# Splitting the next quarter's token norm over the output products, and reading a scan's carry from its own tile

## The chip, the core and the metric

The kernel runs on one NeuronCore of one Trainium2 chip. The metric is the device time of one execution in microseconds (us). Five engines work beside each other, each through its own queue in program order: TensorE (PE, with its weight loads as PEld), VectorE (DVE), ScalarE (ACT), GpSimd (POOL) and SyncE (SP), which here issues nearly all DMAs. They wait for each other by semaphores.

## What is computed

One layer of a hybrid decoder on 2048 tokens of width 1024 with 16 meta tokens in front, all in float32. In short:

```python
xn   = rms_norm(h, norm_w)                    # h: meta tokens, then x
proj = xn @ w_in                              # 72 chunks of 128 columns, and two small ones
o_sb = stick_breaking_attention(q, k, v)      # 4 heads of 128
o_gd = gated_delta_rule_chunked(...)          # 4 heads
o_hg = hgrn2_chunked(...)                     # 4 heads
y    = sum over the three branches b of sigmoid(mix_b) * (o_b @ w_branch[b])
out  = h + y @ w_out
```

In stick-breaking attention a query's weight on a key is sigmoid(z) times the product of sigmoid(-z) over the keys between them. Keys are worked through backwards, block by block, and the running product at a block's first key is the start value (the carry) of the next block:

```python
log_keep   = where(mask, log_sigmoid(-z), 0)
log_passed = cumsum(log_keep, reverse) - log_keep
attn       = where(mask, exp(log_sigmoid(z) + log_passed), 0)
```

## The kernel before

**Tiles and quarters.** Features lie on the 128 partitions, tokens on the free axis. The tokens are worked in four quarters of 512 (`TQ`). A product that needs float32 accuracy is three matmuls (`mm3`, lines 158 to 160): each operand is split into a high part (a cast) and a low part (the rest, by `sub_lo`, line 118). So a weight half of 128x512 is loaded raw (line 146, the tile `wraw`, two buffers), cast on ACT (line 147, `w`), its low part formed on POOL or DVE (line 118), and both parts are written back to device memory for later quarters (line 151, `wk`); from the second quarter on they are loaded ready (line 140).

**A quarter.** `dense_work` yields the dense part in small steps: the projections of attention, delta rule and HGRN2, the gates and products of the three branches (`branch`), and last the output product (`outp`, eight products e = 0 to 7 of 24 matmuls each). The scans of the three branches are separate generators, and `weave` runs them between the steps of the dense part.

**The end of a quarter.** The last branch (b = 2) ends each of its eight products like this: DVE multiplies the PSUM result with the gate (line 1188) and adds y (line 1192), ACT casts the sum to `yh` (line 1194), and POOL forms `yl` (line 118, `S<-D,y`). A PSUM tile of these products is free again after line 1188; `p_acc` has three buffers `acc`, and for part of a quarter one more, `av`. Beside it `norm_stats` loads the next quarter's x (eight tiles `D`) and forms the row factor `rb`. Then `norm_x` (lines 258 to 273) makes the next quarter's normed tokens in one go, eight steps k = 0 to 7, each of three instructions: a multiply on DVE (line 264), a cast to `xh` on ACT (line 269), and the low part `xl` on DVE, or on POOL for k = 2 and 5 (line 118). After it `outp` runs; for each e it loads weights and a piece of x into a tile `D` (line 1215, on SP), adds the finished product on DVE (line 1221) and stores it (line 1222).

**The scan.** `sb_scan` works for each head over blocks of keys; `weights` does, for each of four query tiles i: scores on PE, two sigmoids on ACT into `pc` and `at` (lines 512 and 513), the start value of the block put into the extra column of `pc` by POOL (line 517), a running product over `pc` on DVE (line 518), a copy of its last value, column 0, into a small tile `cc` on DVE (line 523), and the product `at` times `pc` on DVE or POOL (line 526). The scan takes its start value from `cc`, and so does the POOL copy. `pc`, `at` and other tiles share 21 buffers of the pool `S`.

**What sets the order.** The code gives a program order; a scheduler at build time then orders each engine's queue by that order and by a model of when operands and buffers come free. `tc.issue_after(ins)` puts what its block records behind the instruction `ins` in the queue of that instruction's engine; it adds no wait between engines.

Of the kernel before, what the change touches and what calls it, by code (L numbers as in the profile page):

```python
# [7 lines left out]
F32 = mybir.dt.float32  # L8
# [3 lines left out]
ALU = mybir.AluOpType  # L12
# [3 lines left out]
P = 128  # L16
# [23 lines left out]
def kernel(  # L40
# [21 lines left out]
    nc = tc.nc  # L62
# [193 lines left out]
    marks = {}  # L256

    def norm_x(j, xt, rb):

        c0 = META  # L260
        xh, xl = [], []
        for k in range(KC):
            t = xt[k]
            nc.vector.scalar_tensor_tensor(
                t[:, c0:], t[:, c0:], nw[:, k : k + 1], rb[:, c0:], ALU.mult, ALU.mult
            )
            h_ = xpool.tile([P, WQ], F32R, tag=f"xh{k}", name=nm("xh"))
            l_ = xpool.tile([P, WQ], F32R, tag=f"xl{k}", name=nm("xl"))
            nc.scalar.copy(h_[:, c0:], t[:, c0:])
            sub_lo(l_[:, c0:], t[:, c0:], h_[:, c0:], nc.gpsimd if k % 3 == 2 else nc.vector)  # L270
            xh.append(h_)
            xl.append(l_)
        return xh, xl

    CHUNK_US = 5.3
    STEP = 1
# [214 lines left out]
    def sb_scan(j, h, st):  # L491

        qh, ql, kh, kl, vh, vl, vm0, rq, gate = st.pop(h)
        av = p_av()
        carry = [None] * NT
        started = [False]

        def weights(s, lo, hi, skh, skl, ats):
            for i in range(NT):
                e = min(hi, META + (i + 1) * P) if s == j else hi  # L500
                if e <= lo:
                    continue
                n = e - lo
                z = p_z()
                diag = s == j and e == META + (i + 1) * P
                qs = slice(META + i * P, META + (i + 1) * P)
                mm3(z[:, :n], qh[:, qs], ql[:, qs], skh[:, lo:e], skl[:, lo:e], True, not diag)
                if diag:
                    nc.tensor.matmul(z[:, n - P : n], ident_b, neg_b, start=False, stop=True)
                pc = slot("S")  # L510
                at = slot("S")
                nc.scalar.activation(pc[:, :n], z[:, :n], AF.Sigmoid, scale=rq[:, NT + i : NT + i + 1])  # L512
                nc.scalar.activation(at[:, :n], z[:, :n], AF.Sigmoid, scale=rq[:, i : i + 1])  # L513
                if carry[i] is None:
                    nc.gpsimd.memset(pc[:, n : n + 1], 1.0)
                else:
                    nc.gpsimd.tensor_copy(pc[:, n : n + 1], carry[i])
                nc.vector.tensor_tensor_scan(  # L518
                    pc[:, 0:n][:, ::-1], pc[:, 0:n][:, ::-1], zero1.broadcast_to([P, n]),
                    1.0 if carry[i] is None else carry[i], ALU.mult, ALU.add,  # L520
                )
                cc = slot("cc", (P, 1), F32, 10)
                nc.vector.tensor_copy(cc, pc[:, 0:1])
                carry[i] = cc
                eng = nc.gpsimd if i % 2 else nc.vector
                eng.tensor_mul(at[:, :n], at[:, :n], pc[:, 1 : n + 1])  # L526
                ats[i] = at
                yield 0.4 + n * 0.0045

        def values(s, work, svh, svl, vm, final):  # L530
            def product(wi, ath, atl):
                lo, ats, a, kw, kt = work[wi]
                cs_ = slice(kt if (s == j and kt is not None) else 0, None)
                cs_ = slice(cs_.start * P, TQ)
                if kt is None:
                    lh, ll = vm
                else:
                    lh, ll = svh[:, kt * P : (kt + 1) * P], svl[:, kt * P : (kt + 1) * P]
                mm3(
                    av[:, cs_], lh, ll, ath[:kw, cs_], atl[:kw, cs_], not started[0],  # L540
                    final and wi == len(work) - 1,
                )
                started[0] = True

            left = None
            for wi, (lo, ats, a, kw, kt) in enumerate(work):
                i0 = kt if (s == j and kt is not None) else 0
                tr = p_tr()
                for i in range(i0, NT):
                    nc.tensor.transpose(tr[:kw, i * P : (i + 1) * P], ats[i][:, a - lo : a - lo + kw], ident)  # L550
                ath = slot("S", (P, TQ), F32R)
                atl = slot("S", (P, TQ), F32R)
                cs_ = slice(i0 * P, TQ)
                nc.scalar.copy(ath[:kw, cs_], tr[:kw, cs_])  # L554
                sub_lo(atl[:kw, cs_], tr[:kw, cs_], ath[:kw, cs_], nc.vector)
                if left:
                    product(*left)
                left = (wi, ath, atl)
                yield 0.7
            product(*left)  # L560
            yield 0.1

        before = None
        work = []
        for s in range(j, -1, -1):
            vm = vm0
            if s == j:
                skh, skl, svh, svl = kh, kl, vh, vl
            else:
                cs = 0 if s == 0 else META  # L570
                skh = slot("S", dt=F32R)
                skl = slot("S", dt=F32R)
                svh = slot("S", (P, TQ), F32R)
                svl = slot("S", (P, TQ), F32R)
                dd = d_kv[(s, h, "k")] + d_kv[(s, h, "v")]
                for t_, d_ in ((skh, dd[0]), (skl, dd[1])):
                    nc.sync.dma_start(t_[:, cs:].bitcast(F32), d_[:, cs:])
                for t_, d_ in ((svh, dd[2]), (svl, dd[3])):
                    nc.sync.dma_start(t_.bitcast(F32), d_)
                if s == 0:  # L580
                    vm = [slot("vmh", (META, HD), F32R, 2), slot("vml", (META, HD), F32R, 2)]
                    for t_, d_ in zip(vm, dd[4:]):
                        nc.sync.dma_start(t_.bitcast(F32), d_)
            for lo, hi in [(META + 2 * P, WQ), (0, META + 2 * P)] if s == 0 else [(META, WQ)]:
                ats = {}
                now = weights(s, lo, hi, skh, skl, ats)
                if before is None:
                    yield from now
                else:
                    yield from alternate(now, before)  # L590
                if lo == 0:
                    work.append((lo, ats, 0, META, None))
                for kt in range(NT):
                    if lo <= META + kt * P < hi:
                        work.append((lo, ats, META + kt * P, P, kt))
                if s == j == 0 and lo > 0:
                    continue
                if s == j:
                    work.sort(key=lambda w_: -1 if w_[4] == 0 else (0 if w_[4] is None else w_[4]))
                before = values(s, work, svh, svl, vm, lo == 0)  # L600
                work = []
        yield from before
        return put_ob(av, gate)
# [560 lines left out]
    def branch(j, xs, b, obs, y, yh, yl, lag=0):  # L1164
# [10 lines left out]
        def product(e):  # L1175
# [8 lines left out]
            if b == 0:  # L1184
                y[e] = slot("y", (P, TQ))
                nc.vector.tensor_mul(y[e], g, ps)
            else:
                nc.vector.tensor_mul(g, g, ps)  # L1188
                if b == 1:
                    nc.gpsimd.tensor_add(y[e], y[e], g)  # L1190
                else:
                    nc.vector.tensor_add(g, y[e], g)
                    yh[e] = slot("y", (P, TQ), F32R)
                    nc.scalar.copy(yh[e], g)
                    yl[e] = slot("S", (P, TQ), F32R)
                    sub_lo(yl[e], g, yh[e])

        for i in range(KC + lag):
            if i < KC and lag:
# [8 lines left out]
                yield from product(e)  # L1208
            yield END

    def outp(j, yh, yl):
        for e in range(KC):
            wh, wl = load_w(w_out[e], ("out", e))
            xt = slot("D", (P, TQ))
            nc.sync.dma_start(xt, xq[j, :, e, META:])
            ps = p_acc()
            for k in range(KC):
                mm3(ps, wh[k], wl[k], yh[k], yl[k], k == 0, k == KC - 1)
                if k % STEP == STEP - 1 and k < KC - 1:
                    yield 1.3  # L1220
            nc.vector.tensor_add(xt, xt, ps)
            nc.sync.dma_start(out[j, e], xt)
            yield END

# [36 lines left out]
    def dense_work():  # L1261

        xs = norm_x0()
        for j in range(nq):
# [23 lines left out]
            if j + 1 < nq:  # L1288
                xn = norm_stats(j + 1)
            yield from b2  # L1290
            if j + 1 < nq:
                xs = norm_x(j + 1, *xn)
            yield from outp(j, yh, yl)
        flush()

    dense = dense_work()
# [205 lines left out]
```

## Time and profile before

| | |
|---|---|
| median of 3 executions | 2868.03 us (2866.24, 2868.03, 4574.48) |
| profiled execution | 2863.85 us, span of its instructions 2861.6 us |
| granted TensorE clock, mean | 0.995 |
| busy, share of the span | PE 98%, PEld 81%, DVE 53%, ACT 33%, POOL 26% |
| DMA queue of SP | 519.98 MB, 55.9% of 16 engines |
| attention scans | 216, of which 152 start from a carry |
| steps of the norm in question | 3 quarters x 8 |

The profile is of one execution. A group row gives line, engine, operation, tiles (result<-operands), shapes and count, then busy time, mean of one in ns, and the idle time of its engine just before such instructions with what ended it. A row of the waits gives who waited for whom, total us, times and longest. A row of the timeline gives start, duration, engine, line and tiles, with idle time ahead in brackets. A row of a stretch gives its length, the busy time of each engine with the number of instructions, the granted TensorE clock, the share of the DMA engines and GB/s. The busy time of PE is modelled from pipelined matmuls. Line numbers are those of the kernel before; behind the change they are one to five off.

### The profile page before, as it was taken

Reading aid. Unit: us, or ns where it says so; the run is one execution under the profiler, and the core shown is the slowest. Engines: PE = TensorE matmul, PEld = TensorE weight load, DVE = VectorE, ACT = ScalarE, POOL = GpSimd, SP = SyncE. Lnnn points to the kernel's source line nnn. Section 1 sums busy time; section 2 is a strip of 40 time slices with the busy share of each in tenths; the row PEclk is TensorE's granted clock in tenths of the full one; section 3 lists DMA queues with packets and bytes.
Section 4 is the critical chain, followed back from the end, with each engine's and each line's share of the span. In section 5 each row is a group of like instructions: output and inputs, shape, how many; then the busy total and the mean of one; then the engine's idle time right before and its main releaser. Section 6 shows DMA issues by size and latency. Waiting matters only on the chain.

```text
span 2861.6 us, 42199 instructions
## 1 busy us (share of the span) xinstructions
PE 2793.7 (98%) x15720; PEld 2327.8 (81%) x15720; DVE 1523.8 (53%) x3089; ACT 933.8 (33%) x2131; POOL 753.2 (26%) x1009
## 2 busy tenths in 40 slices
PE   7999999998999999999999999999999999999999
PEld 7898788886888888888888878888888777788887
DVE  5466637735357544554156854465415677627521
ACT  5554343243345312113145521211214555112110
POOL 4555213323123401113022321111302233302111
PEclk9999999999999999999999999999999999999999
DMA  6767755667744654446754456344764443653446
GB/s 231 248 210 241 255 174 192 217 233 267 239 164 148 194 178 133 140 148 224 232 192 158 156 163 184 115 140 143 234 227 141 141 140 126 194 156 114 155 148 212
DMA packets 198288, 522.74 MB, mean 183 GB/s; under 512 B 40448, under 2 KB 41536, under 8 KB 198084
## 3 DMA queue, kind: packets, MB, share of 16 engines
q1 hardware_dynamic: 197796, 519.98, 55.9%
q8 instruction: 124, 2.03, 0.3%
q14 instruction: 80, 0.66, 0.1%
q10 hardware_dynamic: 288, 0.07, 0.0%
HBM read 399.13 MB, written 120.84 MB: 182 GB/s over the span
## 4 chain that ended last, share of the span: by engine, by line
PE 82%; DVE 8%; DMA 5%; POOL 2%; ACT 2%; issue 1%; SPq 1%; ACTq 0%; DVEq 0%; POOLq 0%
PE acc L158 18%; PE acc L159 18%; PE acc L160 18%; PE av L158 4%; PE av L159 4%; PE av L160 4%; PE z L1116 2%; PE tr L550 2%; DMA wraw<-in_w_in_dram 2%; PE acc L370 1%; DMA wraw<-in_w_out_dram 1%; DVE D L697 1%; PE z L158 1%; PE z L159 1%; PE z L160 1%
## 5 line engine op out<-in xcount | busy, mean ns | idle before, releaser
L158 PE MATMUL acc<-xh,w 128*128 128x512 f32 (+2 forms) x2248 | 862.3, 384 | 8.5 <-ACT w L147 3.8
L159 PE MATMUL acc<-xl,w 128*128 128x512 f32 (+2 forms) x2248 | 849.4, 378 | 0.3 <-DVE xl L251 0.2
L160 PE MATMUL acc<-xh,w 128*128 128x512 f32 (+2 forms) x2248 | 846.6, 377 | 0.6 <-POOL w L118 0.6
L158 PEld LDWEIGHTS acc<-xh,w 128*128 128x128 f32 x2248 | 426.7, 190 | 83.9 <-ACT w L147 4.3
L160 PEld LDWEIGHTS acc<-xh,w 128*128 128x128 f32 x2248 | 426.6, 190 | 73.9 <-POOL w L118 1.1
L159 PEld LDWEIGHTS acc<-xl,w 128*128 128x128 f32 x2248 | 426.4, 190 | 68.8 <-DVE xl L251 1.3
L118 POOL TENSOR_TENSOR w<-wraw,w 128x512 fp32r<-128x512 f32 x106 | 141.3, 1335 | 301.8 <-ACT w L147 258.7
L526 POOL TENSOR_TENSOR S<-S,S 128x256 f32<-128x256 f32 (+2 forms) x108 | 94.0, 870 | 386.3 <-DVE S L518 229.3
L147 ACT CAST w<-wraw 128x512 fp32r<-128x512 f32 x182 | 112.5, 619 | 248.9 <-DMA wraw<-in_w_in_dram 80.8
L518 DVE TENSOR_TENSOR_SCAN S<-S,cc,zero 128x272 f32<-128x272 f32 (+2 forms) x152 | 144.1, 948 | 82.7 <-ACT S L512 82.3
L512 ACT ACTIVATE S<-z,rq 128x128 f32<-128x128 f32 (+4 forms) x216 | 116.4, 539 | 128.4 <-PE z L160 96.5
L697 DVE SCALAR_TENSOR_TENSOR D<-D,cw,D 128x512 f32<-128x512 f32 (+1 forms) x144 | 125.2, 869 | 22.8 <-ACT D L695 20.5
L158 PE MATMUL acc<-ob,w 128*128 128x512 f32 x316 | 127.3, 404 | 5.3 <-ACT ob L391 3.8
L158 PE MATMUL av<-xh,w 128*128 128x512 f32 (+2 forms) x328 | 129.3, 394 | 0.0
L159 PE MATMUL av<-xl,w 128*128 128x512 f32 (+2 forms) x328 | 128.2, 391 | 0.0
L160 PE MATMUL av<-xh,w 128*128 128x512 f32 (+2 forms) x328 | 127.6, 389 | 0.0
L118 DVE TENSOR_TENSOR S<-tr,S 128x512 fp32r<-128x512 f32 (+4 forms) x176 | 105.3, 606 | 40.2 <-ACT S L554 39.6
L159 PE MATMUL acc<-ob,w 128*128 128x512 f32 x316 | 125.4, 397 | 0.0
L160 PE MATMUL acc<-ob,w 128*128 128x512 f32 x316 | 125.0, 396 | 0.0
L124 POOL TENSOR_SCALAR nu<-nv 128x8 f32<-128x8 f32 (+3 forms) x39 | 15.0, 385 | 407.4 <-DVE nv L993 241.6
L1190 POOL TENSOR_TENSOR y<-y,g 128x512 f32<-128x512 f32 x32 | 47.0, 1473 | 285.8 <-DVE g L1188 285.8
L513 ACT ACTIVATE S<-z,rq 128x128 f32<-128x128 f32 (+4 forms) x216 | 115.9, 537 | 0.0
(380 smaller groups left out, 5209.1 us busy)
## 6 DMA issues: line engine op xcount, KB each, us to landing
w<-wk SPq DMA_DIRECT2D x558, 512.0 KB, 3.6
wk<-w SPq DMA_DIRECT2D x186, 512.0 KB, 3.0
wraw<-in_w_in_dram SPq DMA_DIRECT2D x142, 256.0 KB, 3.6
D<-in_xq_dram SPq DMA_DIRECT2D x56, 256.0 KB, 4.9
S<-rows SPq DMA_DIRECT2D x48, 256.0 KB, 4.8
S<-dv SPq DMA_DIRECT2D x48, 256.0 KB, 4.6
out_dram<-D SPq DMA_DIRECT2D x32, 256.0 KB, 4.5
S<-dk SPq DMA_DIRECT2D x24, 264.0 KB, 4.1
```

What stands on the lines that cost most here:

```text
L118: (eng or nc.gpsimd).tensor_sub(out_, a, hi.bitcast(F32))
L147: nc.scalar.copy(hi, raw)
L158: nc.tensor.matmul(dst, lh, rh, start=first, stop=False)
L159: nc.tensor.matmul(dst, lh, rl, start=False, stop=False)
L160: nc.tensor.matmul(dst, ll, rh, start=False, stop=last)
L512: nc.scalar.activation(pc[:, :n], z[:, :n], AF.Sigmoid, scale=rq[:, NT + i : NT + i + 1])
L513: nc.scalar.activation(at[:, :n], z[:, :n], AF.Sigmoid, scale=rq[:, i : i + 1])
L518: nc.vector.tensor_tensor_scan(pc[:, 0:n][:, ::-1], pc[:, 0:n][:, ::-1], zero1.broadcast_to([P, n]), 1.0 if carry[i] is None else carry[i] ...
L526: eng.tensor_mul(at[:, :n], at[:, :n], pc[:, 1 : n + 1])
L550: nc.tensor.transpose(tr[:kw, i * P : (i + 1) * P], ats[i][:, a - lo : a - lo + kw], ident)
L697: nc.vector.scalar_tensor_tensor(dst[:, c0:], raw[:, c0 + i : c0 + i + n], cw[:, ci, i : i + 1], dst[:, c0:], ALU.mult, ALU.add)
L1116: nc.tensor.matmul(z[:, n * P : (n + 1) * P], kql[:, cs], kql[:, cs], start=True, stop=True)
```

## The change

`norm_x` becomes a generator that stops before each of its eight steps. It is no longer run ahead of `outp`; instead each product e of `outp` runs one step of it, placed in DVE's queue behind the last add recorded there (`marks["y"]`: the add of the branch's last product for e = 0, then the add of the output product before), and in POOL's queue behind the last `yl`. Apart from this, the scan takes its start value from the extra column of its own tile `pc`, which POOL fills from column 0 of the `pc` before it; the tile `cc` and its 216 DVE copies are gone, and a `pc` stays in use until POOL has read it for the next block.

```diff
     def norm_x(j, xt, rb):
         for k in range(KC):
+            yield xh, xl
             t = xt[k]
             nc.vector.scalar_tensor_tensor(
...
-        return xh, xl
+        yield xh, xl
...
                 if carry[i] is None:
                     nc.gpsimd.memset(pc[:, n : n + 1], 1.0)
                 else:
-                    nc.gpsimd.tensor_copy(pc[:, n : n + 1], carry[i])
+                    nc.gpsimd.tensor_copy(pc[:, n : n + 1], carry[i][:, 0:1])
                 nc.vector.tensor_tensor_scan(
                     pc[:, 0:n][:, ::-1], pc[:, 0:n][:, ::-1], zero1.broadcast_to([P, n]),
-                    1.0 if carry[i] is None else carry[i], ALU.mult, ALU.add,
+                    1.0 if carry[i] is None else pc[:, n : n + 1], ALU.mult, ALU.add,
                 )
-                cc = slot("cc", (P, 1), F32, 10)
-                nc.vector.tensor_copy(cc, pc[:, 0:1])
-                carry[i] = cc
+                carry[i] = pc
...
-                    nc.vector.tensor_add(g, y[e], g)
+                    marks["y"] = nc.vector.tensor_add(g, y[e], g).ins
...
-                    sub_lo(yl[e], g, yh[e])
+                    marks["yl"] = nc.gpsimd.tensor_sub(yl[e], g, yh[e].bitcast(F32)).ins
...
-    def outp(j, yh, yl):
+    def outp(j, yh, yl, nx):
+
         for e in range(KC):
             wh, wl = load_w(w_out[e], ("out", e))
+            with tc.issue_after(marks["y"]), tc.issue_after(marks["yl"]):
+                next(nx, None)
             xt = slot("D", (P, TQ))
...
-            nc.vector.tensor_add(xt, xt, ps)
+            marks["y"] = nc.vector.tensor_add(xt, xt, ps).ins
...
+            nx = iter(())
             if j + 1 < nq:
-                xs = norm_x(j + 1, *xn)
-            yield from outp(j, yh, yl)
+                nx = norm_x(j + 1, *xn)
+                xs = next(nx)
+            yield from outp(j, yh, yl, nx)
```

**Place 1, DVE's queue at the end of the first quarter.** L1188 and L1192 are the branch's products (the multiply that frees the PSUM tile, and the add), L264 and `xl` the norm, `w` a low part of a weight half. Before:

```order
L1188 TENSOR_TENSOR D_6965<-D_6965,acc_7312 128x512
L264 SCALAR_TENSOR_TENSOR D_7080<-D_7080,nw,D_7119 128x512
L264 SCALAR_TENSOR_TENSOR D_7082<-D_7082,nw,D_7119 128x512
L264 SCALAR_TENSOR_TENSOR D_7084<-D_7084,nw,D_7119 128x512
L264 SCALAR_TENSOR_TENSOR D_7086<-D_7086,nw,D_7119 128x512
L264 SCALAR_TENSOR_TENSOR D_7088<-D_7088,nw,D_7119 128x512
L264 SCALAR_TENSOR_TENSOR D_7090<-D_7090,nw,D_7119 128x512
L1192 TENSOR_TENSOR D_6965<-y_3709,D_6965 128x512
L264 SCALAR_TENSOR_TENSOR D_7092<-D_7092,nw,D_7119 128x512
L264 SCALAR_TENSOR_TENSOR D_7094<-D_7094,nw,D_7119 128x512
L1188 TENSOR_TENSOR D_7006<-D_7006,av_7345 128x512
L118 TENSOR_TENSOR xl_7437<-D_7080,xh_7436 128x512
```

And now, from the branch's last two products on (L1187 and L1191 are the lines 1188 and 1192 of before, L265 is 264, L1223 the add of an output product, 1221 of before):

```order
L1187 TENSOR_TENSOR D_7132<-D_7132,acc_7349 128x512
L1191 TENSOR_TENSOR D_7132<-y_4314,D_7132 128x512
L118 TENSOR_TENSOR w_1504_7394<-wraw_7395,w_1504_7394 128x512
L1187 TENSOR_TENSOR D_7217<-D_7217,acc_7368 128x512
L1191 TENSOR_TENSOR D_7217<-y_4487,D_7217 128x512
L265 SCALAR_TENSOR_TENSOR D_7032<-D_7032,nw,D_7071 128x512
L118 TENSOR_TENSOR xl_7403<-D_7032,xh_7402 128x512
L118 TENSOR_TENSOR w_1511_7435<-wraw_7436,w_1511_7435 128x512
L1223 TENSOR_TENSOR D_7406<-D_7406,acc_7408 128x512
L265 SCALAR_TENSOR_TENSOR D_7034<-D_7034,nw,D_7071 128x512
L118 TENSOR_TENSOR w_1514_7442<-wraw_7443,w_1514_7442 128x512
L118 TENSOR_TENSOR xl_7451<-D_7034,xh_7450 128x512
```

The eight multiplies of the norm stood ahead of four of the branch's multiplies; now the first stands behind all of them, and each further one behind the add of an output product, with low parts of weights behind it.

**Place 2, ACT's queue at the same spot.** `w` is the cast of a weight half of w_out, `xh` a cast of the norm, `y` a cast of the branch's sum. Before:

```order
L147 CAST w_1516_7390<-wraw_7391 128x512
L269 CAST xh_7436<-D_7080 128x512
L269 CAST xh_7441<-D_7082 128x512
L269 CAST xh_7446<-D_7084 128x512
L269 CAST xh_7451<-D_7086 128x512
L269 CAST xh_7456<-D_7088 128x512
L269 CAST xh_7461<-D_7090 128x512
L1194 CAST y_7327<-D_6965 128x512
L147 CAST w_1541_7475<-wraw_7476 128x512
```

And now:

```order
L147 CAST w_1492_7342<-wraw_7343 128x512
L1193 CAST y_7279<-D_6917 128x512
L1193 CAST y_7312<-D_6958 128x512
L147 CAST w_1501_7387<-wraw_7388 128x512
L1193 CAST y_7331<-D_7072 128x512
L147 CAST w_1504_7394<-wraw_7395 128x512
L1193 CAST y_7364<-D_7132 128x512
L1193 CAST y_7383<-D_7217 128x512
L270 CAST xh_7402<-D_7032 128x512
L147 CAST w_1511_7435<-wraw_7436 128x512
```

The first cast of w_out (`w_1541` before, `w_1501` now) stood behind six casts of the norm and now stands ahead of all of them.

**Place 3, the 112th attention scan, in the third quarter.** DVE before:

```order
L118 TENSOR_TENSOR S_15448<-tr_15444,S_15447 128x256
L518 SCALAR_TENSOR_TENSOR S_15461<-S_15461,cc_15329,zero_380 128x512
L697 SCALAR_TENSOR_TENSOR D_16217<-D_16218,cw,D_16217 128x512
L118 TENSOR_TENSOR S_15494<-tr_15491,S_15493 128x128
L726 TENSOR_SCALAR aq_16062<-nr_16331 128x4
L523 COPY cc_15467<-S_15461 128x1
```

POOL now, up to the copy that fills the extra column of the same scan's tile (`S_15239`), which DVE's scan (now L519, without `cc`) reads:

```order
L518 COPY S_15172<-S_15076 128x1
L518 COPY S_15209<-S_15094 128x1
L525 TENSOR_TENSOR S_15173<-S_15173,S_15172 128x512
L693 COPY halo<-D_15831 128x3
L690 COPY D_15956<-halo 128x3
L518 COPY S_15239<-S_15109 128x1
```

DVE's row L523 is gone, and the scan now waits for the last of these POOL rows and so for what stands ahead of it.

## Prediction

> **What bounds the kernel now.** I begin with the page's busy time by engine, go on to stretches, then to PE's waits, and last to the timelines where a wait lies.
>
> ```profile
> PE 2793.7 (98%) x15720; PEld 2327.8 (81%) x15720; DVE 1523.8 (53%) x3089; ACT 933.8 (33%) x2131; POOL 753.2 (26%) x1009
> ```
>
> PE is busy 2793.7 of 2861.6 us. The change touches no matmul, so it can win only part of the 67.9 us in which PE idles, and what a lowered clock costs beside them. A 2% change, about what a measurement of this kernel can tell from no change, is 57 us. So most of PE's idle time would have to go, and I ask where it lies. The stretches are: up to the end of the first quarter's branches, that quarter's end, the second quarter's end, and the attention of the last quarter.
>
> ```profile
> 0.00:660.00 660.00, 626.46 (x4057) 546.83 (x4058) 378.25 (x781) 278.04 (x641) 255.40 (x297) 0.99 0.66 224
> 660.00:730.00 70.00, 61.18 (x246) 46.57 (x245) 32.73 (x39) 17.11 (x29) 22.84 (x16) 0.95 0.80 275
> 1340.00:1440.00 100.00, 98.63 (x443) 79.56 (x443) 32.48 (x49) 17.14 (x32) 16.99 (x19) 1.00 0.73 237
> 2146.00:2440.00 294.00, 282.26 (x1436) 227.33 (x1434) 202.93 (x364) 154.20 (x316) 87.60 (x144) 0.99 0.42 138
> ```
>
> After the length, the columns are busy time of PE, PEld, DVE, ACT, POOL, then clock and DMA. Half of the idle time (33.5 us) lies ahead of 660, where the norm isn't touched and the change removes only DVE copies. PE idles 8.8 us from 660 to 730, 1.4 us at the second quarter's end, and 11.7 us in the last attention. The waits of PE, over the whole span, then from 640 to 730, then from 1336 to 1410, say on what:
>
> ```profile
> PE acc L158 <- DVE D L1188: 6.9, 2, 6.0
> ...
> PE acc L158 <- DVE D L1188: 6.0, 1, 6.0
> PE acc L160 <- POOL w L118: 1.8, 3, 0.6
> PE acc L158 <- ACT w L147: 1.5, 2, 0.9
> PE acc L160 <- DVE w L118: 0.8, 1, 0.8
> ...
> PE acc L158 <- DVE D L1188: 1.0, 1, 1.0
> ```
>
> Line 1188 frees the PSUM tile of a branch product. PE waits for it twice in the kernel: 6.0 us in the first quarter, 1.0 in the second, not in the third. What DVE does meanwhile is in its timeline, and PE's first rows after the wait show how it starts again:
>
> ```profile
> 658.26 0.68 DVE L1188 TENSOR_TENSOR D<-D,acc 128x512 f32<-128x512 f32 x1
> 658.85 6.15 DVE L264 SCALAR_TENSOR_TENSOR D<-D,nw,D 128x512 f32<-128x512 f32 x6
> ...
> 665.53 2.42 DVE L264 SCALAR_TENSOR_TENSOR D<-D,nw,D 128x512 f32<-128x512 f32 x2
> 667.88 0.68 DVE L1188 TENSOR_TENSOR D<-D,av 128x512 f32<-128x512 f32 x1
> 668.48 3.43 DVE L118 TENSOR_TENSOR xl<-D,xh 128x512 fp32r<-128x512 f32 x3
> 671.83 0.67 DVE L1188 TENSOR_TENSOR D<-D,acc 128x512 f32<-128x512 f32 x1
> 672.65 0.77 PE L158 MATMUL acc<-y,w 128*128 128x512 f32 x1 [5.95 <-DVE D L1188]
> 670.60:677.40 6.80, 4.75 (x11) 3.81 (x12) 6.80 (x12) 1.76 (x3) 1.92 (x2) 0.50 0.56 190
> ```
>
> Between the evictions at 658.26 and 671.83, 12.0 us of norm (6.15 + 2.42 + 3.43) stand in DVE's queue, and PE runs out of PSUM tiles. Its restart falls into 6.8 us at clock 0.50.
>
> **The norm, step by step.** Moving it frees the evictions: the order rows put all eight ahead of the first norm multiply. That removes the 5.95 us. Of the slow stretch PE worked 4.75 us at half speed, so 2.4 us go with it, if the clock stays up. Together **8.4 us** at most in the first quarter.
>
> [...]
>
> What is late next is the loading of w_out, which the first quarter still prepares itself. First the timeline of ACT, then the chain of waits, then the load's own rows:
>
> ```profile
> 666.17 0.61 ACT w L147
> 669.08 1.68 POOL w L118
> 670.78 0.33 SPq L151
> 671.16 3.87 DMA wraw<-in_w_out_dram
> 712.56 4.29 DMA wraw<-in_w_out_dram
> 718.98 0.51 PE acc L160
> L146 SPq DMA_DIRECT2D wraw<-in_w_out_dram x16: 333/423/477, 658.8 to 715.6; - x16
> DMA to landing us min/median/max: 3.5/4.0/5.3
> ```
>
> With two raw buffers the third load waits until the first half's low part is formed. From the third (671.16) to the sixteenth (715.6) take 44.4 us, 3.42 per half, while PE's eight products are paced by it up to a last wait at 718.98. So the end of `outp` moves only as far as the third load moves. That load was late by the norm too: ACT's cast stood behind six norm casts until 666.17, POOL's low part behind norm and `yl` until 669.08. Now the first load (658.8) lands at 662.8 (median 4.0), plus cast 0.61, low part 1.68 and SP's write-back 0.38 (670.78 to 671.16) makes 665.5: **5.7 us** earlier. (In the changed order two pieces of x stand directly ahead of it on SP, four before; I price them at nothing.) I take 6, near this end, as the loads pace what follows; 8.4 would need them faster.
>
> The low end comes from the moved instructions themselves:
>
> ```profile
> L264 DVE SCALAR_TENSOR_TENSOR D<-D,nw,D 128x512 f32<-128x512 f32 x24 | 21.4, 961 | 10.6 <-ACT D L348 10.6
> L118 DVE TENSOR_TENSOR xl<-D,xh 128x512 fp32r<-128x512 f32 x18 | 15.3, 886 | 0.0
> L118 POOL TENSOR_TENSOR xl<-D,xh 128x512 fp32r<-128x512 f32 x6 | 10.4, 1736 | 17.3 <-ACT xh L269 17.3
> ```
>
> Per product the step adds 0.96 us on DVE, a cast on ACT and 0.89 on DVE or 1.74 on POOL, under a product of over 5 us of PE; none of it is a DMA. But DVE's queue is strict: in the changed order the multiplies of steps 1, 2, 3, 5 and 6 stand, behind an output product's add, ahead of weight low parts. If all five lengthen the load chain by 0.96 each (4.8 us), of the 5.7 only 1 is left. So the first quarter's term is −6, between −1 and −8.4. The second quarter loses its 1.0 us wait (its weights come ready), the third nothing. The last step, k = 7, runs beside product 7 and is needed seven eighths into the next projection; without that cover each of three quarter ends would pay one step, at most 0.96 + 0.62 + 0.89 = 2.5 us, but a whole product stands between.
>
> **The scan.** The rows of the copies, one copy in its place, and POOL's side:
>
> ```profile
> L523 DVE COPY cc<-S 128x1 f32<-128x1 f32 x216 | 31.9, 148 | 4.4
> 2310.27 0.14 DVE L523 COPY cc<-S 128x1 f32<-128x1 f32 x1
> 2310.33 0.68 DVE L526 TENSOR_TENSOR S<-S,S 128x512 f32<-128x512 f32 x1
> L517 POOL COPY S<-cc x152: 177/185/1192, 63.6 to 2432.9; 128x1 f32<-128x1 f32 x152
> L125 POOL TENSOR_TENSOR nr<-nu,mhalf 128x8 f32<-128x8 f32 x24 | 44.3, 1844 | 1.8
> PE av L159 <- DVE S L118: 4.3, 5, 2.9
> ```
>
> A copy lasts 148 ns, but the next instruction starts 0.06 us after it, so 216 copies are between 13 and 31.9 us of DVE, a third of them in the last attention. There PE waits 4.3 us for DVE (last row, from 2146 to 2440); elsewhere DVE's time is covered by PE. The new wait, scan for POOL's copy, no row shows. From below: the copy needs only the scan a block earlier, and now skips `cc`. From above: the scan pays for whatever POOL has in hand, 1.84 us if it is the power of a norm. I take **−2** for the scan, half of PE's 4.3; ends −11.7 (all idle of the last attention) and +19 (below). The longer life of four `pc` tiles I price at nothing: PE has no wait of note for a load into `S`, and −2 holds while that is so.
>
> **Sum.** 2863.85 − 6 − 1 − 2 = 2854.85 against the profiled execution (span 2861.6 plus 2.2 around it). The median of the executions shown (2866.24, 2868.03 and one far off) lies 4.2 higher, so I forecast 2868.03 − 9 = **2859**.
>
> **Rivals.**
>
> *The loads take the place of the stall* (first-quarter term −1, scan nothing, second quarter −1): 2866. For it: PE's six waits for a `w` from 640 to 730. Against: ACT and POOL rows above say the loads themselves were held by the norm.
>
> *DVE's relief also empties the last attention:* −6 − 1 − 11.7: 2849. For: DVE is busy 203 of 294 us there and late for PE. Against: ACT and POOL stand in the same waits.
>
> *DVE queues behind POOL, slower than before.* Place: the last attention. Its carry copies, and the scan that shows the mechanism:
>
> ```profile
> 2146.00:2440.00 294.00, 23.09 (x61) 0.99 0.42 138
> 1577.24 1.27 DVE L518 TENSOR_TENSOR_SCAN S<-S,cc,zero 128x512 f32<-128x512 f32 x1
> 1578.47 0.73 POOL L517 COPY S<-cc 128x1 f32<-128x1 f32 x1
> ```
>
> Scan and copy are of one tile: the copy came 1.2 us after the scan had begun, behind a power. The scheduler has reordered this place. Price: the copies' 23.1 us and eight powers (a third of 24) at 1.84, 37.8 us on DVE; PE pays where DVE is full, taken as half of the stretch: +19, with −7 from the norm 2880. It decides from about 0.2 us a scan: 64 scans x 0.2 x half are the 7 us won. Against: POOL is busy only 87.6 of 294 us and mostly itself waits for DVE.
>
> [...]
>
> That the change does not do what it says is excluded for the norm by the order rows.
>
> **How the numbers follow.** Forecast, 2853 to 2864: 0.45. Loads, 2864 to 2868: 0.2. Relief, 2842 to 2853: 0.15. Slower, 2868 to 2885: 0.17. Anything else, a reordering by the scheduler that I have not priced: 0.03. The range 2844 to 2877 leaves out the far ends of relief and slower and the last case, under 2 in 10; the forecast's own is 2853 to 2864. Past 2% either way needs 57 us: faster 0.01, slower 0.02, within 0.97.
>
> **What would show it.** Right: no wait of PE for line 1187 (1188 before) at either border, clock 1.00 around 665 to 680, third load of w_out near 665.5, still 3.4 us a half, `outp` over about 6 us earlier. Wrong: that load near 671, or 3.8 us a half. For the scan: a row DVE L519 <- POOL L518; under 5 us it costs nothing, over 10 in the last attention the slower rival is on. The forecast fails if the idle time of 2146 to 2440 moves by more than 5 us.

## The result and the profile after

The changed kernel takes 2853.52 us (median of 6 executions, 2847.61 to 2855.21) against 2867.77 for the kernel before on the same chip (median of 6, one of them far off at 4574.48): ratio 0.9947, 95% interval 0.9933 to 0.9961. That is 14.3 us faster where 9 were forecast, inside the range, and within 2%. It lies at the very edge of the forecast's own 2853 to 2864. The profiled execution took 2847.61 us (span 2845.8).

The page's busy time, and the four stretches (columns: length, busy time of PE, PEld, DVE, ACT, POOL, then clock, DMA share and GB/s):

```profile
PE 2786.4 (98%) x15720; PEld 2322.3 (82%) x15720; DVE 1498.0 (53%) x2873; ACT 934.2 (33%) x2131; POOL 738.3 (26%) x1009
0.00:660.00 660.00, 624.52 (x4061) 545.48 (x4062) 376.79 (x758) 277.58 (x641) 257.62 (x296) 0.99 0.67 224
660.00:730.00 70.00, 67.77 (x285) 51.60 (x284) 29.56 (x40) 19.21 (x34) 20.45 (x16) 1.00 0.91 313
1340.00:1440.00 100.00, 99.59 (x455) 80.65 (x454) 34.61 (x52) 23.46 (x43) 13.94 (x20) 1.00 0.69 223
2146.00:2440.00 294.00, 282.31 (x1445) 228.00 (x1444) 197.88 (x285) 151.40 (x312) 89.13 (x150) 0.98 0.42 138
```

PE now idles 2.2 us from 660 to 730 (8.8 before) at clock 1.00 (0.95 before), and 11.7 us in the last attention, as before. The waits of PE from 640 to 730 are only two:

```profile
PE acc L160 <- POOL w L118: 1.5, 4, 0.6
PE acc L158 <- ACT w L147: 0.5, 1, 0.5
```

None is for line 1187 (1188 before), nor in the second quarter. DVE's timeline at the first quarter's end shows why, and SP's the third load of w_out:

```profile
661.03 0.91 DVE L1191 TENSOR_TENSOR D<-y,D 128x512 f32<-128x512 f32 x1
663.03 0.69 DVE L1187 TENSOR_TENSOR D<-D,acc 128x512 f32<-128x512 f32 x1 [1.09 <-PE acc L160]
663.75 1.14 DVE L1191 TENSOR_TENSOR D<-y,D 128x512 f32<-128x512 f32 x1
666.78 1.06 DVE L118 TENSOR_TENSOR w<-wraw,w 128x512 fp32r<-128x512 f32 x1 [1.89 <-ACT w L147]
667.77 0.67 DVE L1187 TENSOR_TENSOR D<-D,acc 128x512 f32<-128x512 f32 x1
668.47 1.08 DVE L1191 TENSOR_TENSOR D<-y,D 128x512 f32<-128x512 f32 x1
669.47 0.74 DVE L265 SCALAR_TENSOR_TENSOR D<-D,nw,D 128x512 f32<-128x512 f32 x1
...
666.49 0.39 SPq L146 DMA_DIRECT2D wraw<-in_w_out_dram  x1
...
L146 SPq DMA_DIRECT2D wraw<-in_w_out_dram x16: 333/384/454, 657.9 to 706.3; - x16
```

DVE now waits for PE at the evictions; one norm multiply stands behind the last of them. And the new wait of the scan, over the whole span and then in the last attention:

```profile
DVE S L519 <- POOL S L518: 4.1, 12, 0.4
...
DVE S L519 <- POOL S L518: 2.4, 7, 0.4
```

**Where the time came from.** The table sets PE's matmuls against each other: the times at which `outp` of each quarter starts its first and last matmul, and the matmul number 4001, which stands just ahead of the first quarter's border. Each cell is the time at full clock plus what the stretches at clock 0.50 cost, taken as half their length. That is right where PE is busy in them; where it idles, the cell counts too much clock and too little time, by up to 1.2 us.

| stretch, us | before | after | norm alone | scan alone |
|---|---|---|---|---|
| start to matmul 4001 | 640.1 + 6.8 | 641.0 + 5.1 | 642.3 + 8.5 | 642.8 + 8.5 |
| to the first `outp` | 24.7 + 1.0 | 19.4 + 0 | 19.3 + 0 | 24.4 + 1.1 |
| first `outp` | 49.1 + 2.4 | 49.3 + 0 | 49.6 + 0 | 48.8 + 2.3 |
| to the second | 627.7 + 0 | 626.1 + 0 | 626.3 + 0 | 627.9 + 0 |
| second `outp` to the third | 706.5 + 1.7 | 704.6 + 0 | 706.6 + 1.7 | 704.0 + 1.7 |
| third `outp` to the fourth | 749.9 + 3.4 | 746.6 + 5.1 | 748.2 + 10.2 | 746.7 + 8.5 |

The norm's gain stands in rows 2 to 4: 5.3 us of wait and 3.4 of clock at the first quarter's end, 1.6 at the second's, of which 1.0 is idle time of PE (from 1340 to 1440 it fell from 1.4 to 0.4). The 1.0 of clock in row 2 is really wait: PE stood idle for the first 2.05 us of that slow stretch (670.60 to 672.65). So it is 6.3 us of wait and 2.4 of clock. The scan's gain stands in the last two rows (1.9 and 3.3 us). Of the 3.3 not all need be the scan's, since the norm alone has 1.7 of them. The rest of the difference of two executions is in where the slow stretches fall, of which more below, and in the first row.

### The profile page after: what moved, and what is told of

Read it like the earlier page. It is cut to its first block, busy times and chain, and to the rows that moved or that the text cites. A ratio compares the mean times of both kernels' runs of the same rounds, so it can differ in the third digit from the quotient of the medians.

```text
span 2845.8 us, 42103 instructions
## 1 busy us (share of the span) xinstructions
PE 2786.4 (98%) x15720; PEld 2322.3 (82%) x15720; DVE 1498.0 (53%) x2873; ACT 934.2 (33%) x2131; POOL 738.3 (26%) x1009
## 5 line engine op out<-in xcount | busy, mean ns | idle before, releaser
L519 DVE TENSOR_TENSOR_SCAN S<-S,zero 128x128 f32<-128x128 f32 (+4 forms) x216 | 199.8, 930 | 124.8 <-ACT S L513 112.2
```

The source lines that it names most:

```text
L519: nc.vector.tensor_tensor_scan(pc[:, 0:n][:, ::-1], pc[:, 0:n][:, ::-1], zero1.broadcast_to([P, n]), 1.0 if carry[i] is None else pc[:, n ...
```

## The experiments

**The norm alone and the scan alone.** The first has the changed kernel's norm and the old scan, the second the reverse:

```diff
 # norm_only, against the changed kernel (POOL's copy reads cc again too)
-                    1.0 if carry[i] is None else pc[:, n : n + 1], ALU.mult, ALU.add,
+                    1.0 if carry[i] is None else carry[i], ALU.mult, ALU.add,
...
-                carry[i] = pc
+                cc = slot("cc", (P, 1), F32, 10)
+                nc.vector.tensor_copy(cc, pc[:, 0:1])
+                carry[i] = cc
 # scan_only: this piece the other way round, in the kernel before
```

> Only the norm's part of the change; the scan keeps its copies. If the norm carries nearly all (my theory), PE's lead over the kernel before is 9 to 10 us behind the first quarter's output product and 11 behind the second's, as with the whole change, and the time is 2856 to 2858, ratio 0.996 to 0.9965. If the later 4 to 5 us (won between 1660 and 1770 in the traces) come from the scan, they are missing here. If they come from the norm's timing or from chance, they are here too: 2853, 0.995.

> Only the scan's part: no copies, start value from the scan's own tile. My forecast was 2 us faster (2866, ratio 0.999). If the later gain of the whole change belongs to the scan: 2863, 0.9983, with the short PE wait and the stretch at half clock near 1684 gone. The rival with a slower side, DVE held up by POOL: 2870 or more, with over 10 us of DVE waits for the POOL copy. PE's wait of 6 us for line 1188 stays in all cases.

Measured: norm alone 2860.66 us, ratio 0.9972 (0.9957 to 0.9987); scan alone 2861.16 us, ratio 0.9979 (0.9964 to 0.9994). So the scan brings some 6 us, three times what I had forecast, and the norm some 8 by the ratio, 6.6 by the medians (7.3 us if each time is multiplied by its granted clock: medians 2841.1 against 2848.4; the scan by the same reckoning 5.0). The norm alone is 3 us slower than the 2856 to 2858 expected, the scan alone 2 us faster than the 2863 for the case that the later gain is its own. The two ratios multiply to 0.995, the changed kernel's. The waits of PE from 1640 to 1760 show one place of the scan's gain, first with the norm alone, then with the scan alone:

```profile
PE acc L158 <- ACT ob L392: 1.4, 1, 1.4
PE acc L158 <- DMA w<-wk: 0.7, 1, 0.7
...
PE tr L548 <- POOL S L524: 0.3, 1, 0.3
PE acc L158 <- ACT D L690: 0.2, 1, 0.2
```

The two waits at the third quarter's end, 2.1 us together, are gone with the copies, and that accounts for the 1.9 us of row 5. The first is for the attention's result `ob`. The DVE rows that make it, with the norm alone and with the scan alone, say what it had waited for:

```profile
1674.82 0.69 DVE L389 TENSOR_TENSOR S<-av,D 128x512 f32<-128x512 f32 x1 [5.22 <-PE av L160]
...
1679.21 0.69 DVE L388 TENSOR_TENSOR S<-av,D 128x512 f32<-128x512 f32 x1 [1.79 <-PE av L160]
```

With the copies DVE stood idle for 5.2 us ahead of it, until the last matmul of that product on PE itself. So what held it last was a matmul in PE's queue, and not DVE. PE's build-time order differs in 4182 of 12,732 rows between the changed kernel and one with the copies back (recorded ahead of the run `copy_and_wait` below), though the edit touches no matmul. That is the case that I gave 0.03 as "a reordering by the scheduler that I have not priced". No run here changes PE's order alone, so that the order is the cause is argued, not shown.

**All eight norm steps in one block.**

```diff
             with tc.issue_after(marks["y"]), tc.issue_after(marks["yl"]):
-                next(nx, None)
+                for _ in range(KC if e == 0 else 0):
+                    next(nx, None)
```

> As the changed kernel, but all eight steps of the norm run beside the first output product, still behind the branch's last add. The evictions are free as in the changed kernel. If the evictions and the clock were all that mattered, the time is that of the changed kernel within 1 us (2853.5). If the low parts of the output weights matter, 12 us of norm stand ahead of them in DVE's queue and the ACT casts ahead of theirs: PE then waits for weights in the first quarter's output product and 4 to 8 us come back there (2858 to 2861), and nothing in the second and third quarter, whose weights come ready.

Measured 2860.22 us, ratio 0.9972 (0.9957 to 0.9987), 6 to 8 us above the three medians of the changed kernel (2852.10 to 2854.46, on other chips; its ratios are 0.9935 to 0.9961). The waits of PE at the first border, DVE's timeline, and the stretch that follows:

```profile
PE acc L160 <- DVE w L118: 5.4, 1, 5.4
PE acc L160 <- POOL w L118: 2.0, 4, 0.6
PE acc L158 <- ACT w L147: 1.6, 1, 1.6
...
673.98 7.41 DVE L265 SCALAR_TENSOR_TENSOR D<-D,nw,D 128x512 f32<-128x512 f32 x8
681.32 1.75 DVE L118 TENSOR_TENSOR xl<-D,xh 128x512 fp32r<-128x512 f32 x1
682.99 0.68 DVE L118 TENSOR_TENSOR w<-wraw,w 128x512 fp32r<-128x512 f32 x1
...
681.50:688.30 6.80, 4.58 (x11) 3.61 (x12) 6.38 (x9) 1.17 (x2) 1.23 (x2) 0.50 0.54 193
```

The stall has only moved: the evictions are free, and now a low part of an output weight stands behind 9.0 us of norm (673.98 to 682.99). PE waits 5.4 us for it and starts again at clock 0.50. The first `outp` takes 53.4 + 3.4 us instead of 49.3 to 50.3 in the three profiles of the changed kernel, so the block gives back 6.5 to 7.5 us. Spreading the steps is what keeps the gain, not the place behind the evictions alone.

**Four raw buffers for the output weights.** In the first quarter, every second product's weight halves are loaded into two tiles `g`, free at that time:

```diff
+            raws = None
+            if j == 0 and e % 2:
+                raws = [slot("g", (P, TQ)) for _ in range(2)]
+                for half in range(2):
+                    nc.sync.dma_start(raws[half], w_out[e][:, half * 512 : (half + 1) * 512])
-            wh, wl = load_w(w_out[e], ("out", e))
+            wh, wl = load_w(w_out[e], ("out", e), raws)
```

On the changed kernel, and once more later beside it:

> As the changed kernel, with four raw buffers in place of two for the output weights of the first quarter (every second product's halves go into two tiles of the gates that are free there). My prediction said that the chain of these loads sets the pace of the first quarter's output product. If so, that product, 49.3 us with the change, comes near the 44.4 of the second quarter, and the time is 4 to 5 us shorter (2849). If PE sets the pace and the loads cost only short waits that DMA and casts keep anyway, it is 48 to 49.5 us and the time is unchanged within 1 us.

> The changed kernel with four raw buffers again, now beside the changed kernel on one chip. If the loads of the output weights cost 4.4 us in the first quarter, it is 3 to 5.5 us faster than the changed kernel, ratio to the kernel before 0.992; if the first run's distance was the chip, within 1.5 us.

On the kernel before:

> The kernel before with four raw buffers for the first quarter's output weights and neither part of the change. If these loads cost 4.5 us in that product whatever the norm does, as the run on the changed kernel says, the product shrinks from 51.4 to about 47 (the rest of it is the half clock) and the time is 4 to 5 us shorter, ratio 0.9985. If the norm's stall had covered them there (my rival: loads take the place of the stall), the time is unchanged within 1.5 us.

Measured: on the changed kernel 2847.03 us (ratio 0.992, 0.9896 to 0.9943) and 2848.24 (0.9938, 0.9924 to 0.9953); in the second set the changed kernel itself took 2854.46 (0.9961, 0.9947 to 0.9975), 6.2 us more. On the kernel before 2865.92 (0.9989, 0.9977 to 1.0), 3.5 us less. The first `outp` as one stretch, in the changed kernel, with four buffers, and with four buffers in the kernel before:

```profile
665.55:714.89 49.34, 47.11 (x192) 34.77 (x191) 24.10 (x32) 14.73 (x25) 14.99 (x13) 1.00 0.92 302
...
667.86:712.77 44.91, 44.82 (x192) 35.77 (x191) 23.33 (x32) 14.75 (x25) 15.62 (x13) 1.00 0.97 359
...
679.76:725.56 45.80, 45.80 (x192) 37.00 (x192) 19.42 (x25) 9.64 (x16) 16.59 (x11) 0.97 0.93 339
```

With two buffers the loads cost 4.4 us here with the change (49.3 against 44.9; further profiles read 50.3 against 45.6) and, at full clock, 4.8 without it (49.1 against 44.3, the 45.80 less 1.5 of clock). It is the same toll in both: the norm's stall neither covers it nor is covered by it. This rests on the stretches in the profiles; the time of the kernel before with four buffers is 3.5 us less, short of the 4 to 5 expected, and its interval reaches 1.0. The changed kernel with four raw buffers is the fastest version here.

**The scan's new wait.** Once the scan reads column 0 of the tile before and waits for no POOL copy; once the copies come back while the scan still waits for POOL:

```diff
 # scan_direct, against the changed kernel
-                    1.0 if carry[i] is None else pc[:, n : n + 1], ALU.mult, ALU.add,
+                    1.0 if carry[i] is None else carry[i][:, 0:1], ALU.mult, ALU.add,
 # copy_and_wait, against the changed kernel (POOL's copy reads cc again too)
-                carry[i] = pc
+                cc = slot("cc", (P, 1), F32, 10)
+                nc.vector.tensor_copy(cc, pc[:, 0:1])
+                carry[i] = cc
```

> As the changed kernel, but the scan reads its start value straight from column 0 of the tile before, so it waits for no POOL copy. By my reading of the trace (4.1 us of DVE waits for POOL in 12 places, the longest 0.4 us) that wait costs PE nothing: the time of the changed kernel within 2 us. If the wait costs PE 3 us or more, this one is that much faster. PE's build-time order differs in 2145 rows, so a difference up to 4 us either way can come from that.

> As the changed kernel, but the scan's copies are kept (nobody reads them but POOL) while the scan takes its start value from POOL, so it waits for POOL. PE's build-time order is nearly that of the kernel with the norm alone (462 of 12732 rows differ, 4182 from the changed one). If the new wait costs nothing: the time of the norm alone, ratio 0.997, and the short PE wait near 1680 is back. If the wait costs and the removed copies hid that: 0.999 or more, with over 10 us of DVE waits for POOL.

> The changed kernel again, beside the three others of this set, so that each stands against it on one chip. If part of the first 14 us was chance in where stretches at half clock fall, the ratio comes out nearer to 0.9965, the sum of the two parts' ratios being 0.995; if the parts simply add, 0.995.

Measured on one chip: changed kernel 2852.10 (0.9935, 0.9923 to 0.9948), without the wait 2852.93 (0.9941, 0.9928 to 0.9954), copies and wait 2859.74 (0.9964, 0.9951 to 0.9978). The changed kernel's repeat speaks for parts that simply add (0.995), not for 0.9965. The wait costs nothing that these can tell: taking it away brings nothing, and with the copies back the ratio is that of the norm alone. (Without the wait PE's order is another one too, which by my expectation could hide up to 4 us; but the waits below are short.) DVE's waits at the scan, with copies and wait, and then without the wait:

```profile
DVE S L519 <- ACT S L513: 115.8, 60, 6.0
DVE S L519 <- POOL S L518: 4.4, 12, 1.6
...
DVE S L519 <- ACT S L513: 111.2, 70, 5.9
```

The scan waits for ACT's sigmoids, 26 times as long as for POOL.

**Copies of a constant.** A copy of a constant, written in the code behind each scan, which nothing reads:

```diff
                 carry[i] = pc
+                cc = slot("cc", (P, 1), F32, 10)
+                nc.vector.tensor_copy(cc, zero1)
```

> As the changed kernel, with 216 small copies back on DVE, each right behind a scan, but of a constant, so that nothing waits for the scan's last column through them. PE's build-time order is that of the changed kernel (92 of 12736 rows differ). If the scan's gain is DVE's time, it goes: the stretch from the second to the third quarter's output product takes 662 us again at full clock, the last quarter 705, and the time is 4 to 5 us above the changed kernel. If the gain comes from the order that the scheduler now finds, or from the shorter chain between scans, they stay 660 and 702 and the time is the changed kernel's within 1.5 us.

> The changed kernel, once more beside the others of this set. The stretches at full clock come out as before (first quarter's end 19.3 and 49 to 50 us, then 626, 660 and 702), and the time 2850 to 2855.

Measured 2859.08 us (0.9975, 0.9964 to 0.9985) against 2854.46 for the changed kernel beside it (0.9961, 0.9947 to 0.9975). The copies' group row, then the row of their line with the first and last start, then the stretch from 28 to 56 us here and in the changed kernel:

```profile
L525 DVE COPY cc<-zero 128x1 f32<-128x1 f32 x216 | 14.1, 137 | 0.0
L525 DVE COPY cc<-zero x216: 118/137/147, 30.5 to 52.5; 128x1 f32<-128x1 f32 x108
28.00:56.00 28.00, 24.42 (x151) 21.79 (x150) 22.71 (x242) 13.59 (x27) 15.42 (x18) 0.88 0.61 212
...
28.00:56.00 28.00, 27.11 (x196) 24.87 (x195) 9.20 (x28) 15.44 (x35) 16.06 (x20) 1.00 0.66 225
```

The copies are not where the expectation puts them. They depend on nothing but the constant, and the scheduler has put all 216 at the kernel's start, from 30.5 to 52.5 us, mostly one directly behind the other (14.1 us for 216 that last 137 ns each, near the prediction's lower bound of 13). None runs beside a scan. So this run says nothing on whether the scan's gain is DVE's time. The last two rows of the table stay near the changed kernel's (at full clock 704.3 and 747.8 us; changed kernel in three profiles 703.6 to 704.6 and 745.4 to 746.6; the four kernels with the old copies 706.5 to 706.9 and 748.2 to 750.3), as in a kernel that has no copies there. What the run does show is a price elsewhere: 13.5 us more of DVE from 28 to 56 us leave PE 2.7 us less busy there, at clock 0.88, and up to matmul 4001 the time at full clock is 644.4 us (640.1 to 641.0 in the changed kernel's three profiles). That is enough for the 4.6 us, though the kernel without the wait, which has no copies, also takes 643.3 us there. Whether DVE's time, the chain through the copy or the order of the queues makes the scan's gain stays open.

## Why the prediction was right or wrong

**What bounds.** Right: PE is 98% busy, and the stall at the first border was most of what could be won at the norm. The wait for line 1187 is gone at both borders and the clock around 665 to 680 is 1.00, as the prediction named it.

**First quarter, −6: too small; it was −8.4.** The first sum, 5.95 of wait and 2.4 of clock, came out whole (6.3 of wait ahead of `outp` and 2.4 of clock within it, less 0.3). The slow stretch behind that stall lasted 6.8 us in all three profiles that have the stall (before, scan alone, four buffers before). In its first half PE still idled (2.1 us in the kernel before, from 670.60 to 672.65), and only its second half was busy throughout. The step that failed is "the end of `outp` moves only as far as the third load moves". The third load came at 666.49, near the 665.5 forecast and 4.7 us earlier; the last matmul of `outp` came 9.2 us earlier (724.08 to 714.89); 0.8 of both stems from further ahead (matmul 4001: 646.9 to 646.1). I had spread the loads of before evenly, 3.42 us a half. SP's timeline of before shows that they were not even, and ACT's shows one of the reasons (the third, fifth and seventh load, then two casts):

```profile
671.16 0.42 SPq L146 DMA_DIRECT2D wraw<-in_w_out_dram  x1
...
680.55 0.38 SPq L146 DMA_DIRECT2D wraw<-in_w_out_dram  x1
...
686.43 0.48 SPq L146 DMA_DIRECT2D wraw<-in_w_out_dram  x1
...
681.83 0.62 ACT L1194 CAST y<-D 128x512 fp32r<-128x512 f32 x1 [2.77 <-DVE D L1192]
682.35 0.62 ACT L147 CAST w<-wraw 128x512 fp32r<-128x512 f32 x1
```

From the third (671.16) to the seventh (686.43) they took 3.82 us a half, from there to the sixteenth (715.6) 3.25; after the change, from the third (666.49) to the seventh (679.20), 3.18, and to the last (706.3) 3.06. The other profiles agree: to the seventh 3.83 with the scan alone, which has the stall, and 3.29 with the norm alone, 3.30 and 3.20 in the changed kernel's further two. A cast of a weight half stood behind a cast that waited for an add of the branch, which the norm had made late. So the norm held back four more loads behind the one that I looked at, and that went away with it. This row of casts is one reason that the rows show; the share of others is not known. "Still 3.4 us a half" was wrong, and so was the fear of the multiplies ahead of the low parts: one step at a time costs at most the 1.2 us by which the three profiles of `outp` (49.3 to 50.3 us) exceed the kernel before at full clock (49.1), eight at a time 6.5 to 7.5.

**Second quarter, −1.0:** 1.6 us measured, of which the 1.0 of idle time is the wait that the forecast named. Third, nothing for the norm: its own row agrees (706.5 + 1.7 and 706.6 + 1.7).

**Scan, −2: right sign, wrong place, too small.** 1.9 us lie in the third quarter and up to 3.3 in the last. The half clock at 1684.3 went too (1.7), but that is luck as much: with the scan alone one fell at 1852.3 instead. The idle time from 2146 to 2440 did not move (11.7 us), so the forecast's test held while its reason, DVE's relief in the last attention, did not. The step that failed is "half of PE's 4.3": it looked for the copies' worth in one stretch and in DVE's time there. In the third quarter it was two waits of PE, of which the first, for `ob`, hung on PE's own late matmul while DVE stood idle. What made that matmul late, and what the last quarter's gain is, stays open. As far as the runs show, then, its sign was right by luck and not by its reason. The whole came out 5 us below the forecast because every term was too small.

**Rivals.** Loads taking the place of the stall: out, since the whole 8.4 us came out at the first quarter's end and the loads' toll is the same with and without the stall (4.4 and 4.8 us). DVE behind POOL: out, 4.1 us of waits in all and nothing gained without them. Relief in the last attention: its time was near, its mechanism absent (11.7 us idle before and after).

## What to carry to other kernels

A block of cheap work on an engine that is half idle can cost most of its length where a full engine waits for one instruction behind it (12.0 us of norm cost 8.4, 9.0 cost 6.5 to 7.5); put it in pieces beside long products, since another place for the whole block only changes who waits. To see how far a chain behind a removed stall moves, follow the loads one by one past the stall, not their mean spacing. Where a scheduler sets the order, compare the order of all engines for an edit of 148 ns too: a removed dependency may move more than the time that it took. And where you add an instruction to an experiment, look up in the trace where it ran: 216 copies meant for the whole kernel all ran in its first 53 us.

## What the hardware showed beyond this

In these profiles all stretches at half clock of one execution begin on one grid of 3.413 us, and the grid's phase differs from execution to execution: in the kernel before they begin at 172.2, 339.5, 493.1, 670.6, 1684.3, 2312.4 and 2367.0 us, whole multiples of that apart (443 periods in the 1512.1 us from the first to the fifth), and with the change one begins at 339.2. A window is one period of the grid. Whether a short stall cost clock depended on where it fell. The same stall at the third quarter's end (1.43 us for `ob`, then 0.7 for weights) in two kernels, with the norm alone and with copies and wait; the rows are windows of the grid:

```profile
1674.67:1678.08 3.41, 1.24 (x5) 0.64 (x5) 0.69 (x1) 0.62 (x1) 1.28 (x1) 1.00 0.75 261
1678.08:1681.50 3.42, 3.42 (x10) 2.65 (x9) 1.92 (x2) 0.00 (x0) 0.00 (x0) 0.50 0.14 49
...
1678.10:1681.53 3.43, 2.00 (x9) 1.22 (x7) 0.69 (x1) 0.62 (x1) 0.45 (x1) 1.00 0.45 133
1681.53:1684.94 3.41, 2.72 (x13) 2.02 (x12) 1.17 (x2) 0.00 (x0) 0.83 (x1) 1.00 0.63 174
1684.94:1688.35 3.41, 3.41 (x26) 3.15 (x25) 2.79 (x5) 0.60 (x1) 0.21 (x1) 1.00 0.51 145
```

Where both parts fell into one window (PE idle 2.2 of 3.4 us), the next ran at 0.50; where they fell into two (1.4 and 0.7), none did. Over the 13 profiles of this case, a window at full clock (from the first one granted, about 25 us into the kernel) with 2.0 us or more of PE idle was followed by one at half clock 60 times of 60, with under 0.8 us 2 times of about 10,350, between these 34 of 180. A window at half clock with under 0.8 us of idle was followed by one at full clock 96 times of 111. In the kernel before and the changed kernel alone these are 8 of 8, none of 1605, 3 of 26, and 11 of 11. A stretch lasted one to three windows, 3.4 to 10.2 us. This is most of what differs between executions of one kernel: the 63 executions of the kernel before in three sets spread over 2858 to 2879 us, with standard deviations of 5.3, 4.1 and 4.0 us; time multiplied by clock has 2.1, 2.4 and 2.0, and medians of 2847.2 to 2848.6.
